# Attention loop of a decoder step: the output projection enters one loop step earlier, mixed with the end of the query projections

## The chip, the cores and the metric

One NeuronCore of a Trainium2 chip runs the whole program. The metric is the device time of one launch in microseconds; several launches of a kernel are timed, and their median is what counts. The engines named below are PE (TensorE, the matmuls), DVE (VectorE), ACT (ScalarE), POOL (GpSimd) and SP (SyncE, which here mostly issues DMA transfers). Each engine works through its own instructions in a fixed order; it waits on semaphores where an instruction needs another engine's result or a transfer.

## The reference

One inference step of a two-layer trunk on 1024 new prompt tokens and 8 sample tokens, model width 1024, all in fp32. Every layer has a mixer and a squared-ReLU MLP (width 4096), each behind an RMSNorm and added to the residual stream. Layer 0 mixes with a gated linear recurrence (RG-LRU). Layer 1 mixes with sliding-window attention, 16 query heads over 4 key/value heads of width 64, and that layer is where the change lies:

```python
q, k, v = split(x @ w_qkv)
q, k = rms_norm(q) * q_g, rms_norm(k) * k_g          # per head
s = q @ k.T / 8 - slope[head] * dist                 # keys of the own and the previous block of 128
s = where((dist >= 0) & (dist < 128), s, -1e30)
m = maximum(max(s), sink[head])
p = exp(s - m) / (sum(exp(s - m)) + exp(sink[head] - m))
y = (p @ v) @ w_out                                  # the output projection; then x = x + y
```

## The kernel before, in words

Numbers. Every fp32 product is three passes of a reduced fp32 type: each operand is split into a high part `h` and a low part `l`, and hi·hi, lo·hi and hi·lo are summed. A weight of 128x1024 that comes from DRAM into a `raw` tile is therefore split once: ACT casts the high part (L183, tile `wh`), DVE subtracts it for the low part (L184, tile `wl`), in two halves of 512 columns each. `ensure(i)` runs these splits up to weight i at the place in the program where it is called, and loads the raws of later weights (L177) behind it; a weight that has not been split when a matmul needs it is split at that place.

Tokens are the columns: 1032 of them in three chunks of 344. Activations stand with 128 channels on the partitions, so there are 8 tiles of 128 channels. The query heads are kept in 8 `q` tiles of two heads each.

The attention loop. It has 32 steps g = 0 to 31, `STEPS[g]` = (t, b): a pair of query tiles t and a block b of 128 tokens, 8 blocks for each of 4 pairs. Each step does three things, and they belong to different steps' data:

- `stage_a(g+2)`, two steps ahead (`AHEAD`): the scores, 8 matmuls (L1031) into `bSS`, of which there is a single buffer. POOL computes the distance term (L1034) into a tile `se`, scaled by factors from the query norms; DVE puts masked columns into place (L1038, not in block 0), adds scores and distance term (L1039, out of `bSS` into `se`), takes the maximum (L1040), and ACT does the exponentials (L1044). The next scores can enter `bSS` once L1039 has read it.
- `stage_b(g)`: four PE transposes of the probabilities (L1058) into the single buffer `bT`, read by ACT (L1060) and by DVE (L1062); both write `pt`. At its start POOL takes the difference of two neighbouring value blocks (L1056).
- `stage_c(g-2)`, every second step: probabilities times values and value differences (L1078) into `bO`, split by ACT (L1085) and DVE (L1086). Of the first tiles the result goes to DRAM (`od`), of the last it stays in `oh`/`ol`.

Between these, PE is given other work in small pieces, called fill steps here. `filler()` projects the query tiles 1 to 7 (L938, three matmuls a fill step, 175 fill steps in all). After each projected chunk ACT squares it (L877) and splits it (L879), DVE writes the low part (L880), and SP stores the parts to their `q` tiles (L886, L887). After a tile's last chunk `q_factors` follows: matmuls that sum the squares (L893), an ACT copy (L895), two transposes (L898), and a chain of small DVE and ACT operations (L903, L310 to L313, L315, L907, L908) that ends in the factors which POOL's distance term needs. The factors of the last tile, 7, are first needed by the scores of step 24.

The second source of fill steps, `steps`, is the output projection: for chunk 0 of the tokens and output tiles m = 0 to 3, a group of 6 fill steps over the query tiles 4, 5, 0, 1, 2, 3 (three matmuls each, L244), then the same for chunk 1; tiles 6 and 7 follow after the loop. A group ends with DVE adding the residual (L408, `x`, out of the bank `bP`). The residual tile x[m] comes back from DRAM by an SP transfer (L440), which is issued, with the split of weight wo1[m] if it hasn't been done, when the group m begins (`need(m+1)`). The attention results of tiles 0 to 3 are read back from `od` into `oh`/`ol` by L1183 before that.

What sets the order. Two tables say how many fill steps shall have been taken by which point of the loop, with straight lines between: `FILL` for the query projections up to step `G0`, `EARLY` for the output projection after it. Inside the loop the order of PE's instructions is pinned to the order of the code. For the other engines a scheduler sets the order out of the program order and the dependences, so moving a piece of code can reorder DVE, ACT and SP. Set-up of the output projection, with its L1183 loads, stands behind step G0-1.

Of the kernel before, what the change touches and what calls it, by code (L numbers as in the profile page):

```python
# [13 lines left out]
ALU = mybir.AluOpType  # L14
# [12 lines left out]
NB = SEQ // P  # L27
# [38 lines left out]
def trunk(ctx: ExitStack, tc: tile.TileContext, I, O):  # L66
    nc = tc.nc
    pe, act, dve, pool, sp = nc.tensor, nc.scalar, nc.vector, nc.gpsimd, nc.sync
# [142 lines left out]
    index = {(n, j): k for k, (n, j, _, _) in enumerate(units)}  # L211
    nloaded = [0]

    def ensure(k):
        while nloaded[0] <= min(k, len(units) - 1):
            n, j, _, alloc = units[nloaded[0]]
            fetch(nloaded[0] + (NRAW[int(n[2])] if n[:2] == "dn" else 2))
            if alloc is None:
                loaded[(n, j)] = raws[nloaded[0]]
            else:  # L220
                loaded[(n, j)] = split_unit(raws[nloaded[0]], alloc, pool if nloaded[0] in (3, 13) else dve,
                                            2 if nloaded[0] < 4 or n in ("q", "k", "v", "wo1") else 1)
            nloaded[0] += 1
# [24 lines left out]
    def run(steps):  # L248
        for _ in steps:
            pass  # L250
# [578 lines left out]
    def attention(hs):  # L829
# [123 lines left out]
        def vblk(b, p):  # L953
            h = b // 4
            o = (b % 4) * 256 + p * P
            return v_tiles[h][:, o:o + P]
# [37 lines left out]
        dvs = [se2[1][:, 516 + o:516 + o + P] for o in range(0, 4 * P, P)]  # L994
# [56 lines left out]
        def stage_b(g):  # L1051
            t, b = STEPS[g]
            se, pt = ses[g % 3], B("T")
            y = live["pt", g] = W("pt")
            if b:
                pool.tensor_tensor(dvs[g % 4], vblk(b - 1, t // 4), vblk(b, t // 4), ALU.subtract)  # L1056
            for x in range(4):
                pe.transpose(pt[:, x * P:x * P + P], se[:, x, 0:P], ident)  # L1058
                yield
            act.copy(y[:, 512:1024], pt)  # L1060
            if b:
                dve.tensor_tensor(y[:, 0:512].rearrange("p (x k) -> p x k", x=4), pt.rearrange("p (x k) -> p x k", x=4),  # L1062
                                  four(newer_t), ALU.mult)
            yield
# [136 lines left out]
        fill = filler()  # L1201

        NG = 4 * NB
        AHEAD, G0 = 2, 22
        FILL = {0: 51, 6: 90, 14: 136, G0: 177}
        EARLY = {G0 + 0.3: 0, NG: 48}
        taken = [0]

        def upto(n):
            take(n - taken[0])  # L1210

        def pace(table, g):
            at = max((k for k in table if k <= g), default=min(table))
            to = min((k for k in table if k > g), default=at)
            return table[at] if to == at else table[at] + (table[to] - table[at]) * max(0, g - at) / (to - at)

        def take(n):
            for _ in range(n):
                next(fill, None)
            taken[0] += max(n, 0)  # L1220

        def ready(g):
            t, _ = STEPS[g]
# [11 lines left out]
                run(stage_a(g))  # L1235

        for g in range(NG):
            table = FILL if g < G0 else EARLY
            place = {0: 2, 1: 1}.get((g + AHEAD) % NB, 0)
            with pinned():  # L1240
                if place == 0:
                    scores(g + AHEAD)
                if g != G0:
                    upto(int(pace(table, g + 1 / 3)))
                if g and g % 2 == 0:
                    stage_c(g - 2)
                if g == G0:
                    run(fill)
                    taken[0], fill = 0, steps
                if place == 1:  # L1250
                    scores(g + AHEAD)
                upto(int(pace(table, g + 2 / 3)))
                run(stage_b(g))
                upto(int(pace(table, g + 1)))
                if place == 2:
                    scores(g + AHEAD)
            if g == 17:
                for t in (4, 5):
                    ohl[t] = (A("oh"), A("ol"))
            if 20 <= g < 24:  # L1260
                ensure(index["wo1", g - 20])
            if g == G0 - 1:
                for t in range(4):
                    load_o(t, cs(0))
                for t in (6, 7):
                    ohl[t] = (A("oh"), A("ol"))
                srcs = [ohl[t] for t in range(8)]
                r1 = A("rt")
                rs["r1"] = r1
                xs, need, steps = out_proj("wo1", srcs, spill, "g_mlp1", r1, spill1, before=between, after=ahead(1),  # L1270
                                          early=(4, 5, 0, 1, 2, 3))
                for t in range(4):
                    load_o(t, cs(1))
            if g == 26:
                for t in range(4):
                    load_o(t, slice(2 * CH, SEQ))
# [206 lines left out]
    xs, need, steps = out_proj("wo0", gl, I["xT"], "g_mlp0", r0, spill0, before=lambda m, c: need(m + 1), after=ahead(0))  # L1483
# [146 lines left out]
```

## Time and profile before

| | |
|---|---|
| median of 3 runs | 1963.46 us (1961.69 to 1965.39) |
| the profiled execution, its time and its span | 1962.05 us, 1960.3 us |
| mean granted TensorE clock | 0.996 |
| attention loop | about 1050 to 1235 us of the span |
| PE busy over the span | 1945.4 us, 99% |

The waits list names, for an engine and line, what it waited for: microseconds in total, how many times, the longest. The window view gives a row per stretch: its bounds, its length, then busy time (and instructions) of PE, PEld, DVE, ACT and POOL, then the granted TensorE clock, the share of the DMA engines' time that is busy, and GB/s. Timeline rows have the start, the duration, engine and line, the operation, written tile and read tiles, shapes, and, in brackets, how long the engine stood idle before it and what released it. Matmuls are pipelined: consecutive rows overlap, and the distance of their starts is what one costs.

### The profile page before, as it was taken

To read this page: it belongs to the slowest core of one execution; us is meant where nothing else is said; L and a number is where in the kernel's file an instruction comes from. 1 tells how busy PE (TensorE), PEld (TensorE's weight loads), DVE (VectorE), ACT (ScalarE), POOL (GpSimd) and SP (SyncE) were. 2 spreads that over 40 slices of the span, in tenths; PEclk is the share of its full clock that TensorE was granted. 3 is DMA by queue.
4 is the path that set the end of the run, shared out by engine and by line. 5 is a ranking of instruction groups with operands and counts; after the bars stand their busy time and mean duration, and the time that the engine had idled before them with its cause. 6 is when DMAs were issued, how large, how long until landed. Compare 5 with 4: busy or idle time off the path is not lost.

```text
span 1960.3 us, 34219 instructions
## 1 busy us (share of the span) xinstructions
PE 1945.4 (99%) x12844; PEld 1812.2 (92%) x12844; DVE 1481.4 (76%) x2711; ACT 1008.5 (51%) x1993; POOL 367.8 (19%) x702
## 2 busy tenths in 40 slices
PE   9999999999999999999999999999999999999999
PEld 8999999999999899999999887999999999999998
DVE  8896737987777878778743777579877779687784
ACT  6476635543434555445554676555443436455552
POOL 2330000000000232331032666000000003223321
PEclk9999999999999999999999999999999999999999
DMA  5111242244445788888452345612444447788877
GB/s 184 44 44 54 70 165 83 109 152 157 141 157 177 229 224 236 220 202 206 130 155 81 110 112 191 210 65 103 158 144 150 148 172 263 210 201 216 233 201 181
DMA packets 115909, 308.17 MB, mean 157 GB/s; under 512 B 17560, under 2 KB 46240, under 8 KB 115744
## 3 DMA queue, kind: packets, MB, share of 16 engines
q0 software_dynamic: 30720, 104.18, 22.1%
q1 hardware_dynamic: 54496, 129.36, 20.1%
q10 hardware_dynamic: 30528, 72.45, 10.3%
q8 instruction: 101, 1.65, 0.3%
q14 instruction: 64, 0.52, 0.1%
HBM read 178.08 MB, written 115.16 MB: 150 GB/s over the span
## 4 chain that ended last, share of the span: by engine, by line
PE 92%; DVE 3%; ACT 2%; DMA 1%; issue 1%; POOL 1%; SPq 0%; DVEq 0%; ACTq 0%
PE bD L609 36%; PE bZ L609 26%; PE bP L244 11%; PE bS L244 7%; PE bT L244 3%; PE bP L938 3%; PE bSS L1031 1%; PE bO L1078 1%; PE bS L968 1%; PE bT L1058 1%; DMA x<-xT 1%; ACT se L1044 0%; DVE wl L184 0%; DMA raw<-w_out 0%; DVE sq L295 0%
## 5 line engine op out<-in xcount | busy, mean ns | idle before, releaser
L609 PEld LDWEIGHTS bD<-op,op 128*128 128x128 f32 x3072 | 380.5, 188 | 7.9
L609 PE MATMUL bD<-op,op 128*128 128x260 f32 x3072 | 383.0, 282 | 0.0
L609 PEld LDWEIGHTS bD<-tl,op 128*128 128x128 f32 x2880 | 362.4, 188 | 11.6 <-DVE ho L757 0.3
L609 PE MATMUL bD<-tl,op 128*128 128x260 f32 x2880 | 366.4, 282 | 0.1
L622 POOL DMA_DIRECT2D tl<-hsum x210 | 125.4, 682 | 886.9 <-PE bD L609 785.4
L456 ACT CAST op<-ws 128x512 fp32r<-128x512 f32 (+2 forms) x288 | 158.7, 561 | 246.9 <-DVE ws L577 114.8
L609 PE MATMUL bZ<-op,op 128*128 128x512 f32 x1152 | 282.2, 394 | 0.0
L609 PE MATMUL bZ<-tl,op 128*128 128x512 f32 x1080 | 271.8, 394 | 0.2 <-DVE tl L464 0.2
L609 PEld LDWEIGHTS bZ<-op,op 128*128 128x128 f32 x1152 | 210.4, 188 | 43.6 <-ACT he L743 0.2
L609 PEld LDWEIGHTS bZ<-tl,op 128*128 128x128 f32 x1080 | 194.4, 188 | 37.7 <-DVE tl L464 0.7
L464 DVE TENSOR_TENSOR tl<-tl 128x520 fp32r<-128x520 f32 (+1 forms) x210 | 136.4, 692 | 77.1 <-ACT tl L463 76.9
L456 ACT CAST op<-raw 128x512 fp32r<-128x512 f32 (+2 forms) x216 | 120.9, 562 | 133.9 <-PE bD L609 73.0
L457 DVE TENSOR_TENSOR op<-ws,op 128x512 fp32r<-128x512 f32 (+2 forms) x288 | 171.5, 610 | 7.3 <-ACT op L456 7.1
L457 DVE TENSOR_TENSOR op<-raw,op 128x512 fp32r<-128x512 f32 (+2 forms) x216 | 131.7, 611 | 9.3 <-ACT op L456 8.5
L757 DVE TENSOR_TENSOR ho<-bD,ho 128x520 f32<-128x520 f32 x140 | 97.5, 697 | 37.1 <-PE bD L609 36.2
L463 ACT CAST tl<-tl 128x520 fp32r<-128x520 f32 (+1 forms) x210 | 117.5, 626 | 2.1 <-DVE ho L674 0.7
L184 DVE TENSOR_TENSOR wl<-raw,wh 128x512 fp32r<-128x512 f32 (+1 forms) x73 | 63.6, 890 | 34.7 <-ACT wh L183 18.1
L747 DVE TENSOR_TENSOR ho<-bZ,ho 128x512 f32<-128x512 f32 x72 | 49.6, 689 | 44.2 <-PE bZ L609 44.0
L731 ACT COPY he<-bZ 128x512 f32<-128x512 f32 x72 | 42.0, 583 | 75.3 <-PE bZ L609 69.8
L757 DVE TENSOR_TENSOR he<-bD,he 128x520 f32<-128x520 f32 x71 | 49.4, 696 | 40.6 <-PE bD L609 40.3
L749 ACT COPY he<-bZ 128x512 f32<-128x512 f32 x68 | 39.9, 587 | 77.0 <-PE bZ L609 64.9
L183 ACT CAST wh<-raw 128x512 fp32r<-128x512 f32 (+1 forms) x76 | 57.2, 775 | 36.2 <-PE bT L244 11.3
(371 smaller groups left out, 3839.4 us busy)
## 6 DMA issues: line engine op xcount, KB each, us to landing
raw<-w_up SPq DMA_DIRECT2D x64, 512.0 KB, 3.8
tl<-hsum POOLq DMA_DIRECT2D x120, 260.0 KB, 6.7
raw<-w_dn SPq DMA_DIRECT2D x64, 384.0 KB, 6.2
tl<-hsum POOLq DMA_DIRECT2D x90, 256.0 KB, 6.3
spill<-ho POOLq DMA_DIRECT2D x32, 516.0 KB, 6.9
spill<-he POOLq DMA_DIRECT2D x32, 516.0 KB, 6.3
hsum<-ts ACTq DMA_DIRECT2D x30, 520.0 KB, 4.0
hsum<-ho ACTq DMA_DIRECT2D x30, 516.0 KB, 3.5
```

The lines of the kernel that those rows point to most:

```text
L183: act.copy(r_(hi[:, sl]), raw[:, sl])
L184: eng.tensor_tensor(r_(lo[:, sl]), raw[:, sl], hi[:, sl], ALU.subtract)
L244: pe.matmul(o, lhsT=r_(wt[:, col(k):col(k) + P]), rhs=r_(xt[:, cs(c)]), start=(k == first and a == 0), stop=(k == final and a == 2))
L456: act.copy(r_(hi), x)
L457: dve.tensor_tensor(r_(lo), x, hi, ALU.subtract)
L463: act.copy(r_(hi), lo)
L464: eng.tensor_tensor(r_(lo), lo, hi, ALU.subtract)
L609: pe.matmul(d[:, 512 * b:512 * b + c], lhsT=r_(wt[:, j * P:j * P + P]), rhs=r_(xt[:, c * b:c * b + c]), start=first and j == 0 and a == 0, ...
L622: pool.dma_start(t[:, n:2 * n], src)
L747: dve.tensor_tensor(o0, d, o[:, HP], ALU.add)
L757: last["sum"] = dve.tensor_tensor(t, inner(d), t, ALU.add).ins
L938: pe.matmul(o, lhsT=r_(wt[:, k * P:k * P + P]), rhs=r_(xt[:, cs(c)]), start=(k == 0 and a == 0), stop=(k == M8 - 1 and a == 2))
```

## The change

- `G0` goes from 22 to 21, so the output projection is set up, with its loads L1183, behind step 20 and enters the loop in step 21.
- In step G0 the kernel before ran all that was left of the query projections at once (`run(fill)`) and then went over to `steps`. Now both are merged: `mixed` takes one fill step of the one, then one of the other, until the query projections are through, and `steps` alone after that. The table for that step's end is `EARLY`.
- The numbers of `FILL` and `EARLY` are others: 92 instead of 90 fill steps at step 6, 139 instead of 136 at step 14, 176 at step 21.3; six steps of the merged source by step 22, 48 at the end of the loop.
- The splits of wo1[0] to wo1[3] are asked for behind the steps 20, 22, 24 and 26, not 20, 21, 22 and 23.
- POOL's difference of two value blocks is taken for the next step, behind the transposes, not for the own step ahead of them. Its line is L1059 now; the transposes' line is L1056.

```diff
@@ stage_b
-            if b:
-                pool.tensor_tensor(dvs[g % 4], vblk(b - 1, t // 4), vblk(b, t // 4), ALU.subtract)
             for x in range(4):
                 pe.transpose(pt[:, x * P:x * P + P], se[:, x, 0:P], ident)
                 yield
+            if (g + 1) % NB:
+                pool.tensor_tensor(dvs[(g + 1) % 4], vblk(b, t // 4), vblk(b + 1, t // 4), ALU.subtract)
             act.copy(y[:, 512:1024], pt)
@@ the loop
-        AHEAD, G0 = 2, 22
-        FILL = {0: 51, 6: 90, 14: 136, G0: 177}
-        EARLY = {G0 + 0.3: 0, NG: 48}
+        AHEAD, G0 = 2, 21
+        FILL = {0: 51, 6: 92, 14: 139, G0 + 0.3: 176}
+        EARLY = {G0 + 0.4: 0, G0 + 0.7: 3, G0 + 1: 6, NG: 48}
...
+        def mixed(a, b):
+            for _ in a:
+                yield
+                next(b)
+            yield from b
...
-            table = FILL if g < G0 else EARLY
+            table = FILL if g <= G0 else EARLY
...
-                if g != G0:
-                    upto(int(pace(table, g + 1 / 3)))
+                upto(int(pace(table, g + 1 / 3)))
                 if g and g % 2 == 0:
                     stage_c(g - 2)
                 if g == G0:
-                    run(fill)
-                    taken[0], fill = 0, steps
+                    taken[0], fill, table = 0, mixed(fill, steps), EARLY
...
-            if 20 <= g < 24:
-                ensure(index["wo1", g - 20])
+            if g in (20, 22, 24, 26):
+                ensure(index["wo1", (g - 20) // 2])
```

What that does to the order of instructions, at three places. In these rows a tile's name carries a buffer number; `x2` says that a row stands for two such instructions.

DVE where the output projection begins. Before, with wl_13129 the low part of wo1[1], wl_13240 that of wo1[2], and x_13190 the residual tile x[0]:

```order
L1062 TENSOR_TENSOR pt_13111<-bT_13110,side_10405 128x512
L184 TENSOR_TENSOR wl_13129<-raw_13055,wh_13128 128x512 x2
L903 TENSOR_TENSOR qs_13179<-bN_13119,st 128x16
L1046 RECIPROCAL den_10401<-den_10401 128x4
L1086 TENSOR_TENSOR ol_12838<-bO_13163,oh_12837 128x256
L1062 TENSOR_TENSOR pt_13197<-bT_13196,side_10405 128x512
...
L908 RECIPROCAL st<-st 128x16
L1039 TENSOR_TENSOR se_10407<-bSS_13211,se_10407 128x4x128
...
L408 TENSOR_TENSOR x_13190<-bP_13192,x_13190 128x344
```

The same place with the change; wl_13195, wl_13300 and wl_13413 are the low parts of wo1[1], wo1[2] and wo1[3], x_13147 is x[0]:

```order
L1062 TENSOR_TENSOR pt_13154<-bT_13153,side_10405 128x512
L903 TENSOR_TENSOR qs_13174<-bN_13140,st 128x16
L408 TENSOR_TENSOR x_13147<-bP_13149,x_13147 128x344
L184 TENSOR_TENSOR wl_13195<-raw_13065,wh_13194 128x512 x2
L1046 RECIPROCAL den_10401<-den_10401 128x4
...
L908 RECIPROCAL st<-st 128x16
L184 TENSOR_TENSOR wl_13300<-raw_13192,wh_13299 128x512 x2
L1086 TENSOR_TENSOR ol_12875<-bO_13206,oh_12874 128x256
L1062 TENSOR_TENSOR pt_13223<-bT_13222,side_10405 128x512
L1086 TENSOR_TENSOR ol_12877<-bO_13206,oh_12876 128x256
L184 TENSOR_TENSOR wl_13413<-raw_13297,wh_13412 128x512 x2
L1039 TENSOR_TENSOR se_10407<-bSS_13237,se_10407 128x4x128
```

The split of wo1[1] moved from ahead of the first group's residual add L408 to behind it, and three weights' splits now stand within eleven instructions, the last of them directly ahead of the add L1039 that frees `bSS`.

PE there, with the change (bP_13149 is the bank of group m = 0, bP_13202 that of m = 1). Before, the 4 matmuls L893 were followed by stage_c (L1078), L898 and then group 0, and scores stood between the groups:

```order
L1031 MATMUL bSS_13102<-kl_10745,q_12192 128x256
L893 MATMUL bN_13140<-sq_12860,con 32x256 x4
L244 MATMUL bP_13149<-oh_12874,wh_13067 128x344
...
L1056 MATMUL bT_13153<-con,se_10407 128x128 x4
...
L898 MATMUL bN_13140<-con,qc_13141 128x128 x2
...
L244 MATMUL bP_13149<-oh_13085,wl_13068 128x344
L244 MATMUL bP_13202<-oh_12874,wh_13194 128x344
L244 MATMUL bP_13202<-ol_12875,wh_13194 128x344
L244 MATMUL bP_13202<-oh_12874,wl_13195 128x344
L1078 MATMUL bO_13206<-pt_13051,vt_10403 64x256 x2
```

Group 0, the transposes of step 21 and the end of the query factors are woven into one another, all 18 matmuls of group 0 and three of group 1 stand ahead of stage_c of step 20, and the third of group 1 reads wl_13195.

DVE at a block 0 in the middle of the loop, and near its end. Before, the L184 pair of that query weight stood 15 instructions later, and the mask copy of the late scores was followed by L1062:

```order
L1062 TENSOR_TENSOR pt_11982<-bT_11981,side_10405 128x512
L1039 TENSOR_TENSOR se_10408<-bSS_11996,se_10408 128x4x128
...
L1038 COPY_PREDICATED bSS_13499<-side_10405,bSS_13499 128x4x128
L1062 TENSOR_TENSOR pt_13477<-bT_13476,side_10405 128x512
L1039 TENSOR_TENSOR se_10408<-bSS_13499,se_10408 128x4x128
```

With the change:

```order
L1062 TENSOR_TENSOR pt_11989<-bT_11988,side_10405 128x512
L184 TENSOR_TENSOR wl_12076<-raw_11752,wh_12075 128x512 x2
L1039 TENSOR_TENSOR se_10408<-bSS_12003,se_10408 128x4x128
...
L1038 COPY_PREDICATED bSS_13514<-side_10405,bSS_13514 128x4x128
L1046 RECIPROCAL den_10400<-den_10400 128x4
L1039 TENSOR_TENSOR se_10408<-bSS_13514,se_10408 128x4x128
L1062 TENSOR_TENSOR pt_13492<-bT_13491,side_10405 128x512
```

A split of a query weight stands ahead of the add that frees `bSS`, and late in the loop the read of `bT` stands behind that add instead of ahead of it.

## The prediction

> **What bounds the kernel now.** I read the busy times first, then PE's waits, then windows and timelines around the two waits that lie in the attention loop.
>
> ```profile
> PE 1945.4 (99%) x12844; PEld 1812.2 (92%) x12844; DVE 1481.4 (76%) x2711; ACT 1008.5 (51%) x1993; POOL 367.8 (19%) x702
> PE bSS L1031 <- DVE se L1039: 4.3, 2, 3.5
> PE bO L1078 <- DVE pt L1062: 1.3, 1, 1.3
> ```
>
> PE is the bound. The change removes no matmul and adds none, so only PE's waits and its clock can move. Inside the loop PE waits 5.6 us on DVE. Most of that is in one place, where the output projection begins:
>
> ```profile
> 1186.97 0.65 PE L1078 MATMUL bO<-pt,se 128*64 128x256 f32 x4 [1.30 <-DVE pt L1062]
> 1191.22 0.32 PE L244 MATMUL bP<-ol,wh 128*128 128x344 f32 x1
> 1191.38 0.32 PE L244 MATMUL bP<-oh,wl 128*128 128x344 f32 x1
> 1195.16 0.58 PE L1031 MATMUL bSS<-kh,q 128*128 128x256 f32 x1 [3.47 <-DVE se L1039]
> ...
> 1193.21 0.25 DVE L908 RECIPROCAL st<-st 128x16 f32<-128x16 f32 x1
> 1194.42 0.69 DVE L1039 TENSOR_TENSOR se<-bSS,se 128x512 f32<-128x512 f32 x1 [0.95 <-POOL se L1034]
> ```
>
> The 3.47 us are the chain of tile 7's factors: L908 ends at 1193.46, POOL's distance term follows, DVE's add then frees the scores' only buffer. What comes behind the wait is in the windows:
>
> ```profile
> 1187.50:1191.70 4.20, 4.20 (x31) 3.84 (x29) 2.66 (x8) 2.95 (x12) 2.87 (x7) 1.00 0.97 277
> 1191.70:1194.30 2.60, 0.00 (x0) 0.00 (x0) 1.72 (x5) 0.50 (x1) 0.67 (x2) 1.00 1.01 404
> 1194.30:1201.10 6.80, 5.94 (x24) 5.88 (x25) 5.21 (x12) 3.65 (x11) 3.75 (x13) 0.50 1.02 383
> ```
>
> After 2.60 us without a matmul the granted clock falls to 0.50 and stays there for 6.80 us. PE is busy for 5.94 of them at half speed, so 2.97 us are lost. The DMA engines are full here (0.97 to 1.02), which will matter.
>
> **What the change takes away.** With the query projections' end mixed into step 21, tile 7's factors start about one step earlier against the scores that need them, and stage_c of step 20 stands behind group 0 rather than directly behind the transposes. Both waits lose their cause: 1.30 + 3.47 = 4.77. With the 3.47 goes its half-clock stretch, 2.97. **Gain: 7.74 us**, if nothing takes their place.
>
> **C1, the wait of group m = 1 for wo1[1]'s low part.** This is the largest cost. The order rows show that DVE makes wl_13195 behind the residual add L408 of group 0. That add needs x[0], whose SP transfer is issued only when group 0 begins; before the change the low part was made ahead of all that. When does PE reach the third matmul of group 1? Take PE's old track and correct it by what now stands elsewhere:
>
> ```profile
> 1184.16 0.65 PE L1078 MATMUL bO<-pt,vt 128*64 128x256 f32 x4
> 1187.56 0.44 PE L898 MATMUL bN<-con,qc 128*128 128x128 f32 x2
> 1188.31 0.60 PE L1058 MATMUL bT<-con,se 128*128 128x128 f32 x4
> 1188.66 0.41 PE L244 MATMUL bP<-oh,wh 128*128 128x344 f32 x1
> 1189.70 0.22 PE L1031 MATMUL bSS<-kh,q 128*128 128x128 f32 x1
> 1190.54 0.37 PE L244 MATMUL bP<-oh,wh 128*128 128x344 f32 x1
> ```
>
> The 15th projection matmul of the old track ends its slot at 1191.38 + 0.16 = 1191.54. Away go the wait (1.30), stage_c (1187.56 - 1184.16 - 1.30 = 2.10), one set of transposes (0.35) and the scores (0.84); five more projection matmuls come in (20 stand before the waiting one), 5 x 0.16 = 0.80. PE arrives at 1187.75.
>
> And the low part?
>
> ```profile
> 1178.24 0.53 SPq L1183 DMA_DIRECT2D ol<-od0l  x1
> 1183.08 0.43 SPq L1183 DMA_DIRECT2D oh<-od2h  x1
> L440 SPq DMA_DIRECT2D x<-spill x8: 319/376/384, 1188.7 to 1227.0; - x8
> DMA to landing us min/median/max: 3.9/5.5/7.5
> 1198.13 0.52 DVE L408 TENSOR_TENSOR x<-bP,x 128x344 f32<-128x344 f32 x1 [0.16 <-PE bP L244]
> 1182.80 1.31 DVE L184 TENSOR_TENSOR wl<-raw,wh 128x512 fp32r<-128x512 f32 x2
> ```
>
> SP's queue is in order, and in the changed program a row of 13 of the loads L1183 stands directly ahead of x[0]. Ten steps from 1178.24 to 1183.08 take 4.84, 0.48 each; 13 of them bring x[0]'s issue to 1184.5. These transfers land 3.9 to 7.5 us after issue, median 5.5; with the DMA engines full I take 6.0, so x[0] is there at 1190.5. The add (0.52 here) and two halves of the split (1.31) follow: 1192.3. C1 is therefore 4.55 less whatever has delayed PE before (C2): with the bounds of the landing 2.45 to 6.05 for both together.
>
> **C2, the last squares.** L893 reads the squares of tile 7's last chunk. On ACT these stand behind a copy out of `bT`, a cast of stage_c and both halves of wo1[0]'s cast:
>
> ```profile
> 1183.75 0.59 ACT L1060 COPY pt<-bT 128x512 f32<-128x512 f32 x1
> 1188.01 0.35 ACT L1085 CAST oh<-bO 128x256 fp32r<-128x256 f32 x1
> 1181.54 1.15 ACT L183 CAST wh<-raw 128x512 fp32r<-128x512 f32 x2
> 1183.02 0.46 ACT L877 ACTIVATE sq<-bP 128x344 f32<-128x344 f32 x1 [0.33 <-PE bP L938]
> ```
>
> That is 0.59 + 0.35 + 1.15 + 0.46 = 2.55 from the transposes on, while PE has six projection matmuls (0.96) and eight scores to do (0.12 apart at full width, 0.96), 1.92. The difference and some 0.3 until a copy starts give 0.9, bounds 0 and 1.6. It is no cost on top: C1 shrinks by it, to 3.65. **C1 + C2 = 4.55.**
>
> **C3, scores of step 25.** From the transposes of step 22 on, DVE waits about 1.0 for ACT's copy, as the 0.59 of the copy and its start make it, and then has L1062, L1086, two halves of a split and the scores' add: 0.7 + 0.4 + 1.3 + 0.7, together 4.1 us. PE has nine projection matmuls (1.44), the narrow scores of step 24 (0.84) and three more (0.48), 2.76 us, before the next scores: a wait of 1.4. If the clock is halved there, PE takes 5.5 and the wait is nil. I take 0, bound 1.4.
>
> **C4, late transposes.** In one late step DVE now does L1039 before it reads `bT`:
>
> ```profile
> 1216.94 0.67 DVE L1038 COPY_PREDICATED bSS<-side,bSS 128x512 f32<-128x512 int32 x1
> 1217.52 0.68 DVE L1062 TENSOR_TENSOR pt<-bT,side 128x512 f32<-128x512 f32 x1
> 1218.12 0.68 DVE L1039 TENSOR_TENSOR se<-bSS,se 128x512 f32<-128x512 f32 x1
> 1218.35 0.63 PE L1058 MATMUL bT<-con,se 128*128 128x128 f32 x4
> ```
>
> Already now the transposes start 0.15 after L1062's end (1218.20). With L1039 and a reciprocal between, that end moves 0.7 later, and PE, with three projection matmuls fewer in between, comes 0.48 sooner: 1.2 to 1.4. I take 1.3, bounds 0 and 1.4.
>
> **C5, splits of query weights.** At scores 8 PE has no slack at all:
>
> ```profile
> 1108.74 0.68 DVE L1039 TENSOR_TENSOR se<-bSS,se 128x512 f32<-128x512 f32 x1
> 1109.47 0.39 PE L1031 MATMUL bSS<-kh,q 128*128 128x256 f32 x1
> 1137.62 1.40 DVE L184 TENSOR_TENSOR wl<-raw,wh 128x512 fp32r<-128x512 f32 x2
> ```
>
> The next scores start 0.05 after the add's end. The new order puts a pair of halves ahead of such an add (1.3), and another pair ahead of a mask copy further on, where more PE work lies between (0.8, half of it covered). Together 2.1, bounds 0 and 2.8.
>
> **C6, the clock again.** A wait of 3.65 is longer than the 2.60 of empty PE behind which the clock fell. 1.05 us of a halved stretch of 6.80 would then pass in the wait, 5.75 in work: 2.9 lost, bounds 0 and 3.4. The Trainium skill ("TensorE: Matmul & The Clock Gate", section "HAM oscillation — how this bites in real kernels") puts the limit at idle gaps of more than about 3.4 us; the gap of this trace, 3.47, is just above it. By that figure C6 would be paid as well, but only just.
>
> POOL's value difference costs nothing: POOL is busy 19%, and the product that reads it comes at least a step later. If that cover were gone, it would be one such instruction per step ahead of the distance term.
>
> **Sum.** -7.74 + 4.55 + 0 + 1.3 + 2.1 + 2.9 = +3.1. Against the profiled execution's own 1962.05 us that is 1965.2; this execution lies 1.4 below the median of the runs, so **I forecast 1966.6 us**.
>
> **Rivals.** *The clock holds.* If x[0] lands in the median 5.5, C1 is 3.15, and if the clock then isn't lowered, C6 is nil and C3 is paid: -7.74 + 4.05 + 1.4 + 1.3 + 2.1 = +1.1, 1964.6. Against it speaks the fall after 2.60 us of no work, and another one that needed no empty PE at all:
>
> ```profile
> 1275.79 2.40 PE L1152 MATMUL bN<-ssb,vc 128*128 128x8 f32 x20
> 1279.60:1286.50 6.90, 6.90 (x28) 6.90 (x27) 2.48 (x12) 1.75 (x6) 0.00 (x0) 0.51 0.07 27
> ```
>
> Twenty tiny matmuls preceded it. The page's limit would separate 3.15 from 3.65, so by it this case is a matter of half a microsecond in the landing of one transfer.
>
> *DVE is early (faster).* If x[0] lands after 3.9, as the fastest did, the low part is ready at 1190.2, C1 + C2 is 2.45 and the clock holds; if the pairs of halves then also meet an idle DVE (busy 76%), C4 and C5 vanish: -7.74 + 2.45 + 1.4 = -3.9, 1959.6. It decides at a wait of less than 2.6 in group 1. The missing slack at scores 8 speaks against it.
>
> *The loads come late (slower by more).* Three raws of w_out and the x tiles are now wanted within one step, on DMA engines that are full. If x[0] needs 7.5, C1 + C2 is 6.05; and if wo1[2]'s raw takes the longest time that this kind took, the splits ahead of L1086, L1062 and L1039 stand about 2 us longer and all of DVE's queue with them:
>
> ```profile
> DMA to landing us min/median/max: 3.1/4.5/8.5
> ```
>
> That row is of the raws, L177: 8.5 against 4.5. +3.1 + 1.5 + 2.0 = +6.6, 1970.1. For it speak the 404 GB/s of the empty stretch; against it, that the loads of `oh`/`ol` start a step earlier and so free the queue earlier.
>
> That the change doesn't do what it says is excluded for the mixing (the order shows it), but not for the splits: called two steps apart, they still stand within eleven DVE instructions.
>
> **How the numbers follow.** Forecast 0.46, the clock holds 0.17, DVE early 0.22, loads late 0.15. A measurement here can't tell less than about 0.2%, 3.9 us, from no change: faster is below 1959.5, slower above 1967.4. The forecast's own range, 1964 to 1969, lies 0.28 within and 0.18 above; the clock's case is within (0.17); DVE early sits on the lower bound (0.13 faster, 0.09 within); late loads are above (0.14, 0.01 within). Faster 0.13, the same 0.55, slower 0.32. The range runs from 1959.5 to 1970, which leaves out about half of either outer case, 0.2 in all.
>
> **What would show it.** Right: no wait of L1031 on L1039 in step 22 above 1 us and none of L1078; a wait of 3 to 4 us of PE at L244 in group 1, released by DVE's L184; x[0]'s L440 issued near 1184.5 less the earlier gains, landing after the group's last matmul; a clock of about 0.5 behind it; waits of L1031 near scores 8, of the transposes late. Wrong: group 1 without a wait (x[0] early, or the low part ahead of L408 after all), or a granted clock of 1.00 through the whole loop.

## The result

The changed kernel takes 1970.01 us (median of 7 runs, 1966.91 to 1972.92); the kernel before, timed on the same chip in the same rounds, 1963.12 us (7 runs, 1960.59 to 1965.39). The ratio is 1.0035, 95% interval 1.0023 to 1.0047: slower by 6.9 us, 0.35%, clear of no change. The forecast was 1966.6 us, 3.1 more than the kernel before, and the range ran from 1959.5 to 1970: the measured time lies on its upper end. The direction was right, the rise more than twice the forecast one, and of the prediction's own chances a loss that can be seen had 0.32, none that can be seen 0.55.

The profiled execution of the changed kernel took 1968.33 us, its span is 1966.5 us, 6.2 more than the span before. PE's busy time is the same to 0.4 us, and its waits are others. First the busy times and the list of PE's waits with the change:

```profile
PE 1945.8 (99%) x12844; PEld 1808.4 (92%) x12844; DVE 1481.2 (75%) x2711; ACT 1007.4 (51%) x1993; POOL 364.2 (19%) x702
...
PE bP L244 <- DVE wl L184: 5.0, 1, 5.0
PE bSS L1031 <- DVE se L1039: 2.9, 3, 1.2
PE bT L1056 <- DVE pt L1062: 1.9, 2, 1.3
...
PE bN L893 <- ACT sq L877: 0.7, 1, 0.7
...
PE bT L1056 <- DVE q L313: 0.4, 1, 0.4
```

The two waits that the kernel before had at the output projection's beginning, 1.30 and 3.47 us, are gone. In their place stands one of 5.0 us, on the instruction that the prediction named: the third matmul of group 1, for wo1[1]'s low part. In the timelines of PE, DVE and SP:

```profile
1191.51 0.31 PE L244 MATMUL bP<-ol,wh 128*128 128x344 f32 x1
1196.81 0.66 PE L244 MATMUL bP<-oh,wl 128*128 128x344 f32 x1 [4.98 <-DVE wl L184]
1205.62 0.38 PE L1031 MATMUL bSS<-kh,q 128*128 128x256 f32 x1 [1.23 <-DVE se L1039]
...
1195.04 0.52 DVE L408 TENSOR_TENSOR x<-bP,x 128x344 f32<-128x344 f32 x1 [3.72 <-DMA x<-spill]
1195.47 1.28 DVE L184 TENSOR_TENSOR wl<-raw,wh 128x512 fp32r<-128x512 f32 x2
...
1187.51 0.38 SPq L440 DMA_DIRECT2D x<-spill  x1
```

It is read from the bottom up: x[0] is asked for at 1187.51 and lands 7.4 us later; DVE stands at L408 for 3.72 us and starts it at 1195.04, 7.5 us after the issue; then come the add and the two halves of the split, and PE goes on at 1196.81. The windows show the clock behind it (length, then busy PE, PEld, DVE, ACT, POOL; granted clock; DMA share; GB/s):

```profile
1187.80:1191.80 4.00, 4.00 (x28) 3.71 (x26) 3.42 (x9) 3.13 (x9) 1.57 (x5) 1.00 0.97 327
1191.80:1193.90 2.10, 0.03 (x1) 0.00 (x0) 0.00 (x0) 1.46 (x7) 0.00 (x0) 1.00 1.09 244
1193.90:1200.70 6.80, 3.89 (x17) 2.01 (x17) 3.89 (x10) 1.14 (x2) 3.58 (x10) 0.50 0.84 269
```

The clock fell 2.1 us into the wait and was half for 6.8 us again, but 2.9 of these passed in the wait itself.

The waits ahead of step 20 and late in the loop, in PE's timeline, with the two rows of DVE that make the first of them wait, a split ahead of the add that frees `bSS`:

```profile
1111.69 0.39 PE L1031 MATMUL bSS<-kh,q 128*128 128x256 f32 x1 [0.98 <-DVE se L1039]
1129.38 0.65 PE L1078 MATMUL bO<-pt,se 128*64 128x256 f32 x4 [0.24 <-DVE pt L1062]
1147.06 0.63 PE L1056 MATMUL bT<-con,se 128*128 128x128 f32 x4 [0.37 <-DVE q L313]
1155.60 0.39 PE L1031 MATMUL bSS<-kh,q 128*128 128x256 f32 x1 [0.73 <-DVE se L1039]
1177.60 0.63 PE L1056 MATMUL bT<-con,se 128*128 128x128 f32 x4 [0.59 <-DVE pt L1062]
...
1226.22 0.63 PE L1056 MATMUL bT<-con,se 128*128 128x128 f32 x4 [1.32 <-DVE pt L1062]
1294.42 0.43 PE L244 MATMUL bP<-ol,wh 128*128 128x344 f32 x1 [0.44 <-DVE ol L272]
...
1109.75 1.28 DVE L184 TENSOR_TENSOR wl<-raw,wh 128x512 fp32r<-128x512 f32 x2
1110.95 0.68 DVE L1039 TENSOR_TENSOR se<-bSS,se 128x512 f32<-128x512 f32 x1
```

### The profile page after: what moved, and what is told of

Read it like the earlier page. It is cut to its first block, busy times and chain, and to the rows that moved or that the text cites. A ratio compares the mean times of both kernels' runs of the same rounds, so it can differ in the third digit from the quotient of the medians.

```text
span 1966.5 us, 34229 instructions
## 1 busy us (share of the span) xinstructions
PE 1945.8 (99%) x12844; PEld 1808.4 (92%) x12844; DVE 1481.2 (75%) x2711; ACT 1007.4 (51%) x1993; POOL 364.2 (19%) x702
## 4 chain that ended last, share of the span: by engine, by line
PE 91%; DVE 4%; ACT 2%; DMA 1%; issue 1%; SPq 0%; POOL 0%; ACTq 0%; DVEq 0%
PE bD L609 36%; PE bZ L609 26%; PE bP L244 11%; PE bS L244 7%; PE bT L244 3%; PE bP L938 3%; PE bO L1078 1%; PE bSS L1031 1%; PE bS L968 1%; ACT se L1044 1%; PE bT L1056 1%; DVE wl L184 1%; DMA raw<-w_in 1%; DVE sq L295 0%; DMA tl<-hsum 0%
## 5 line engine op out<-in xcount | busy, mean ns | idle before, releaser
L184 DVE TENSOR_TENSOR wl<-raw,wh 128x512 fp32r<-128x512 f32 (+1 forms) x73 | 63.6, 888 | 36.6 <-ACT wh L183 19.9
```

The lines of the kernel that those rows point to most:

```text
L184: eng.tensor_tensor(r_(lo[:, sl]), raw[:, sl], hi[:, sl], ALU.subtract)
```

## The experiments

Eleven kernels were run. They were timed in three groups, each with the kernel before beside them on the same chip; its medians there were 1963.23, 1963.60 and 1963.37 us, and a ratio is to the kernel before of the same group. Single runs of one kernel scatter by 4 to 10 us, so that a difference of less than about 2 us between two kernels can't be told. The question was which part of the change costs what, and whether it is an order on DVE (theory A) or full DMA engines that make something late anyway (theory B).

### The split of wo1[1] asked for earlier

```diff
             if g in (20, 22, 24, 26):
-                ensure(index["wo1", (g - 20) // 2])
+                ensure(index["wo1", max(1, (g - 20) // 2)])
```

> The changed kernel with the split of wo1[1] asked for behind step 20, together with wo1[0]'s, so that DVE makes its low part ahead of the residual add L408. Theory A (order: the low part of wo1[1] stands behind L408, which waits for x[0]): the 5.0 us wait of L244 on L184 goes, with it the half clock behind it (about 2.0 us), and, since DVE's order there changes too, the 1.2 us of L1031 in the next step and the 1.3 us of the late transposes: about 9.5 us less, 1960.5 us. Theory B (transfers: the DMA engines are full there, so PE will wait for the next thing that comes late, wo1[2]'s raw or the attention results): the wait moves to group 2 or to the oh/ol tiles and keeps 3 us or more, with the half clock; less than 4 us gained, 1966 us or more.

Measured: 1968.05 us, 1.0022 of the kernel before (1.0013 to 1.0031). The 5.0 us wait is gone, as both theories of its cause had it, but only about 2 us of time with it, hardly more than can be told. PE waits at other places: 1.76 us for the last squares (L893), which now stand behind two more halves of a cast on ACT, 1.61 us at the scores of step 25, 1.15 at late transposes. The profiled execution is the slowest of the eleven (1971.57 us); in it the scores of step 9 wait 2.71 us, a part of it for a transfer issue on ACT (below, under hardware), and a half clock of 3.4 us follows that wait and another the 1.76 us. Theory A was right on the wait, wrong on the time. The time is theory B's, but not in its way: no wait of 3 us or more stands at group 2 or at the `oh`/`ol` tiles.

### x[0] asked for earlier

```diff
+                need(1)
                 for t in range(4):
                     load_o(t, cs(1))
```

> The changed kernel with x[0]'s load issued ahead of the second row of eight loads L1183, so some 3.8 us earlier; DVE's order is as in the changed kernel. Theory A: x[0] lands 3.8 us earlier, the wait of L244 on L184 shrinks from 5.0 to about 1.2 us, no half clock behind it: 5.8 us less, 1964.2 us. Theory B: on full DMA engines an earlier issue lands hardly earlier; the wait stays above 3.5 us and the time within 2 us of the changed kernel's 1970.

Measured: 1966.15 us, 1.0016 (1.0006 to 1.0025). In this kernel's profile:

```profile
1184.15 0.38 SPq L440 DMA_DIRECT2D x<-spill  x1
...
1191.38 0.52 DVE L408 TENSOR_TENSOR x<-bP,x 128x344 f32<-128x344 f32 x1
...
1193.15 0.42 PE L244 MATMUL bP<-oh,wl 128*128 128x344 f32 x1 [1.50 <-DVE wl L184]
1201.41 0.39 PE L1031 MATMUL bSS<-kh,q 128*128 128x256 f32 x1 [2.54 <-DVE se L1039]
...
1196.03 1.14 ACT L183 CAST wh<-raw 128x512 fp32r<-128x512 f32 x2 [2.72 <-DMA raw<-w_out]
```

Only the issue was moved, by 3.4 us, and the wait fell from 4.98 to 1.50 with no half clock behind it: x[0]'s place in SP's queue is what made group 1 wait. So far theory A; what theory B expected, an early issue that lands hardly earlier, did not come, since x[0] took 5.1 us to land here and 7.4 in the changed kernel. But the scores of step 25 now wait 2.54 us instead of 1.23, and a half clock of 3.4 us follows: ACT stands 2.72 us for the raw of wo1[2], DVE's split of it follows, and behind that split stands the add for the scores. ACT's wait for that raw is not new, it is 4.18 us in the changed kernel; there PE itself came to these scores 5.5 us later (1204.39 instead of 1198.87). By the medians some 3.9 us of the expected 5.8 came; the rest was given back to the transfer that is late next.

### The old pace of the query projections

```diff
-        FILL = {0: 51, 6: 92, 14: 139, G0 + 0.3: 176}
+        FILL = {0: 51, 6: 90, 14: 136, G0 + 0.3: 176}
```

> The changed kernel with the pace of the query projections as before: 90 fill steps at step 6 and 136 at step 14, where the change has 92 and 139. All else as changed. The splits of the query weights are again where they were, behind the scores' add; and in the order that the scheduler then makes, wo1[1]'s low part stands ahead of L408, and the read of bT late in the loop ahead of L1039. Theory A: the waits of 0.98, 0.24, 0.37 and 0.59 us in the steps before 20 go (2.1 us), the 5.0 with its half clock (2.0), the 1.2 and the 1.3 too: about 11.5 us less, 1958.5 us, faster than the kernel before. Theory B: only the 2.1 us in the early steps go, the transfers keep PE waiting in groups 1 and 2: 1967 us.

Measured: 1961.09 us, 0.9993 (0.9984 to 1.0002), no difference from the kernel before that can be told; against the changed kernel's 1.0035 that is some 8 us less. Two numbers of the pace undo the whole loss, with the mixing, the later splits and the moved value difference all left in. The 5.0 us are 0.73 us here, since the low part stands ahead of L408 in DVE's order. Three larger waits are left: 2.00 us at the scores of step 9 behind a slow issue on ACT (below, under hardware), 1.16 at the late transposes, for POOL (L1048) now instead of L1062, and 2.57 at the scores of step 25 again. The rows of the order and of the last of these:

```profile
1188.93 1.28 DVE L184 TENSOR_TENSOR wl<-raw,wh 128x512 fp32r<-128x512 f32 x2
1193.25 0.52 DVE L408 TENSOR_TENSOR x<-bP,x 128x344 f32<-128x344 f32 x1 [3.04 <-PE bP L244]
...
1195.04 1.14 ACT L183 CAST wh<-raw 128x512 fp32r<-128x512 f32 x2 [2.05 <-DMA raw<-w_out]
1195.69 1.29 DVE L184 TENSOR_TENSOR wl<-raw,wh 128x512 fp32r<-128x512 f32 x2 [0.74 <-ACT wh L183]
1197.84 0.68 DVE L1039 TENSOR_TENSOR se<-bSS,se 128x512 f32<-128x512 f32 x1
1198.58 0.38 PE L1031 MATMUL bSS<-kh,q 128*128 128x256 f32 x1 [2.57 <-DVE se L1039]
```

The expected 1958.5 is missed by 2.6 us; theory A had none of these three waits.

### The value difference back at its old place

```diff
+            if b:
+                pool.tensor_tensor(dvs[g % 4], vblk(b - 1, t // 4), vblk(b, t // 4), ALU.subtract)
             for x in range(4):
...
-            if (g + 1) % NB:
-                pool.tensor_tensor(dvs[(g + 1) % 4], vblk(b, t // 4), vblk(b + 1, t // 4), ALU.subtract)
```

> The changed kernel with POOL's value difference at its old place, at the start of the step that uses it. Theory: POOL is busy 19% and nothing of the product waits for this difference; DVE's order stays as changed, so 1970 us, within 1 us. Rival: the difference ahead of the transposes delays POOL's distance term and so the scores' add, or its move was what freed it: 2 us or more either way.

Measured: 1971.24 us, 1.0032 (1.0022 to 1.0041), the same as the changed kernel, with the same waits (4.42, 1.22, 1.32 us). In the changed kernel this part costs and brings nothing that can be measured.

### The new pace alone, on the kernel before

```diff
-        FILL = {0: 51, 6: 90, 14: 136, G0: 177}
+        FILL = {0: 51, 6: 92, 14: 139, G0: 177}
```

> The kernel before with nothing but the changed pace of the query projections: 92 fill steps at step 6 and 139 at step 14 instead of 90 and 136. DVE's order in the early steps is then that of the changed kernel, a pair of L184 halves ahead of the scores' add. Theory A: PE waits of about 1.0, 0.2, 0.4 and 0.6 us appear in the steps before 20, and the two old waits at the start of the output projection stay: 2.1 us more than before, 1965.3 us. Rival: the early waits only take PE time that the later 1.3 and 3.5 us waits would take anyway (the chain of tile 7's factors then has more room): no difference, 1963 us.

Measured: 1968.01 us, 1.0026 (1.0015 to 1.0038): 4 to 5 us slower, most of the change's loss by itself and more than either theory had. The early waits are there (1.08, 0.23, 0.37 us, then 0.51 and 0.54 at two transposes). They are 2.7 us together by the list; by PE's progress they cost more, since the first matmul of group 0, with the same work done before it in both kernels, starts at 1191.72 instead of 1187.75, 4.0 us later. And the old wait of 3.47 us grew by 1.4:

```profile
1195.33 0.62 ACT L183 CAST wh<-raw 128x512 fp32r<-128x512 f32 x1 [2.74 <-DMA raw<-w_out]
...
1195.98 0.69 DVE L184 TENSOR_TENSOR wl<-raw,wh 128x512 fp32r<-128x512 f32 x1 [3.19 <-ACT wh L183]
1196.96 0.23 DVE L313 SCALAR_TENSOR_TENSOR q<-qs,st,q 128x16 f32<-128x16 f32 x1
1198.60 0.25 DVE L908 RECIPROCAL st<-st 128x16 f32<-128x16 f32 x1
1200.54 0.58 PE L1031 MATMUL bSS<-kh,q 128*128 128x256 f32 x1 [4.88 <-DVE se L1039]
...
1189.70 0.53 SPq L177 DMA_DIRECT2D raw<-w_out  x1
```

Here the chain of tile 7's factors (L313 to L908) stands behind a half of wo1[2]'s split, which waits for that weight's raw. In the kernel before, its first operation stood ahead of that half:

```profile
1190.50 0.43 DVE L313 SCALAR_TENSOR_TENSOR q<-qs,st,q 128x16 f32<-128x16 f32 x1
1191.71 0.69 DVE L184 TENSOR_TENSOR wl<-raw,wh 128x512 fp32r<-128x512 f32 x1 [0.77 <-ACT wh L183]
```

The raw was issued at 1189.70; before it was at 1185.12. There are two raw buffers, so wo1[2]'s raw can be asked for only when wo1[0]'s split is through, and with the new pace that split ends at 1188.1 instead of 1184.1. But PE is 4.0 us later there as well: against PE the half of the split starts only 0.3 us later. The other 1.1 us are order: from the start of that half to the end of L908 DVE takes 2.87 us instead of 1.75, with L1086, L313 and the read of `bT` (L1062) between them now. So it is again the order on DVE, more than the transfer, that links the pace of the earlier steps with a wait in step 22.

### The splits again one step apart, with the old pace

```diff
-            if g in (20, 22, 24, 26):
-                ensure(index["wo1", (g - 20) // 2])
+            if 20 <= g < 24:
+                ensure(index["wo1", g - 20])
```

> As the changed kernel with the old pace, and also with the splits of wo1[0] to wo1[3] asked for behind the steps 20, 21, 22 and 23 as before. What is left of the change is the mixing in step 21 with its earlier set-up, and POOL's value difference. Theory A: the first two splits stand where they stood with the old pace alone, so the same waits at group 1 (0.7 us) and at the scores of step 25 (2.6 us with a half clock of 3.4 us behind it): the same time, 1961 us. Rival: the splits two steps apart are what leaves the scores of step 25 waiting; then 2 to 4 us less, 1957 to 1959 us.

Measured: 1961.94 us, 0.9995 (0.9987 to 1.0004); waits of 0.70 us in group 1 and 2.54 at the scores of step 25. As theory A has it, the distance of the splits does nothing here.

### The splits a step earlier, with the old pace

```diff
-            if g in (20, 22, 24, 26):
-                ensure(index["wo1", (g - 20) // 2])
+            if 19 <= g < 23:
+                ensure(index["wo1", g - 19])
```

> As the changed kernel with the old pace, and the splits of wo1[0] to wo1[3] asked for behind the steps 19, 20, 21 and 22. The two raw buffers come free a step earlier, so that the raws of wo1[1] and wo1[2] are loaded ahead of the rows of loads L1183 and behind x[0]. Theory A (the wait of 2.6 us of step 25's scores is DVE held up by the split of wo1[2], whose raw lands late): that wait falls below 1 us and its half clock goes, about 3.5 us less than with the old pace alone: 1957.5 us. Theory B (the DMA engines are full, so a load moved ahead makes another late): a wait of 2 us or more elsewhere in steps 21 to 25, 1961 us.

Measured: 1960.59 us, 0.9988 (0.9980 to 0.9997): by its interval just faster than the kernel before. In its profile, in step 21 and after:

```profile
1179.64 0.38 SPq L177 DMA_DIRECT2D raw<-w_out  x1
...
1190.41 1.42 DVE L184 TENSOR_TENSOR wl<-raw,wh 128x512 fp32r<-128x512 f32 x2 [0.53 <-ACT wh L183]
1194.80 1.31 DVE L184 TENSOR_TENSOR wl<-raw,wh 128x512 fp32r<-128x512 f32 x2 [0.47 <-ACT wh L183]
...
1184.94 0.63 PE L893 MATMUL bN<-sq,con 128*32 128x256 f32 x4 [1.38 <-ACT sq L877]
1196.77 0.39 PE L1031 MATMUL bSS<-kh,q 128*128 128x256 f32 x1 [1.51 <-DVE se L1039]
```

With wo1[0] split earlier its buffer is free earlier, wo1[2]'s raw is issued at 1179.64, and its split (1190.41) no longer holds up the scores' add; the one that stands ahead of that add now is wo1[3]'s (1194.80). The wait fell from 2.57 to 1.51 and no half clock follows. The last squares wait more for it (1.38 instead of 0.43). Between the two theories: the named wait shrank by the named cause, yet not below 1 us, and against the old pace alone the gain, 0.5 us by the medians, can't be told from none.

### wo1[0] split two steps earlier, with the old pace

```diff
-            if g in (20, 22, 24, 26):
-                ensure(index["wo1", (g - 20) // 2])
+            if g in (18, 20, 21, 22):
+                ensure(index["wo1", {18: 0, 20: 1, 21: 2, 22: 3}[g]])
```

> As the changed kernel with the old pace, and the splits of wo1[0] to wo1[3] asked for behind the steps 18, 20, 21 and 22. Same question as in the run with 19, 20, 21 and 22, with wo1[0]'s raw buffer free another step earlier; in DVE's order a half of wo1[3]'s split stands ahead of the add that the scores of step 25 wait for. Theory A: 1 us for that half, else as there: 1958.5 us. Theory B: 1961 us.

Measured: 1961.36 us, 0.9987 (0.9979 to 0.9996), the same as the run before it and theory B's number, with 1.61 us at the scores of step 25. These two are the only kernels of the study whose interval lies below the kernel before: by 0.12 and 0.13%, some 2.5 us, with upper ends of 0.9997 and 0.9996.

### One number of the pace at a time

```diff
-        FILL = {0: 51, 6: 92, 14: 139, G0 + 0.3: 176}
+        FILL = {0: 51, 6: 90, 14: 139, G0 + 0.3: 176}
```

> The changed kernel with 90 fill steps at step 6 as before, but still 139 at step 14. In DVE's order the early pairs of L184 stand behind the scores' add again, except one half ahead of a mask copy, while the low part of wo1[1] still stands behind L408, wo1[3]'s still ahead of the add of step 24, and the late read of bT still behind L1039. Theory A: the early waits (0.98, 0.24, 0.37, 0.59 us) go, the 5.0 with its half clock, the 1.2 and the 1.3 stay: 2 us less than the changed kernel, 1968 us. Rival (the early waits are what makes the later ones, by bringing PE and the loads out of step): 1963 us or less.

```diff
-        FILL = {0: 51, 6: 92, 14: 139, G0 + 0.3: 176}
+        FILL = {0: 51, 6: 92, 14: 136, G0 + 0.3: 176}
```

> The changed kernel with 136 fill steps at step 14 as before, but 92 at step 6. Here DVE's order keeps the pair of L184 ahead of the add of scores 8, while wo1[1]'s low part stands ahead of L408 and the late read of bT ahead of L1039, as with the old pace. Theory A: the wait of about 1.0 us at scores 9 stays, the 5.0 us go and the others are as with the old pace: 1 us above that one's 1961, 1962.3 us. Rival: 1967 us or more.

Measured: 1967.19 us, 1.0022 (1.0013 to 1.0031), with only step 6 back; 1965.39 us, 1.0010 (1.0001 to 1.0020), with only step 14 back. The first is theory A's number, the second lies between its theory and its rival. The order on DVE separates as expected: in the first the wait of L244 for L184 stays (4.66 us), in the second it is 0.72 us. So it is the number at step 14 that puts wo1[1]'s low part behind L408, with no edit near that place. The early waits don't separate so cleanly. In the first kernel they were expected to go and stayed in other places (0.81 and 0.60 us at transposes, 0.90 at scores); in the second there are more of them than expected (0.59, 0.80, 0.34). In both profiles a slow issue on ACT adds to the wait at the scores of step 9 (1.31 and 2.31 us). What the pace costs early in the loop, and at which scores, is left open in detail.

### The new pace with the splits a step earlier

```diff
-            if g in (20, 22, 24, 26):
-                ensure(index["wo1", (g - 20) // 2])
+            if 19 <= g < 23:
+                ensure(index["wo1", g - 19])
```

> The changed kernel with its new pace, and the splits of wo1[0] to wo1[3] asked for behind the steps 19, 20, 21 and 22. DVE makes the low part of wo1[1] well ahead of L408 then; one half of wo1[2]'s stands behind it. Theory A: the early waits stay (2.1 us), the 5.0 us with its half clock go, the scores of step 25 wait about 1.5 us: what the same splits gave with the old pace (1960.6) and 2.1 on top, 1962.7 us. Rival (the pace itself costs more than its early waits): 1966 us or more.

Measured: 1966.70 us, 1.0022 (1.0012 to 1.0031), the rival's number. Group 1 no longer waits. The transfer of x[0] holds DVE all the same, and the wait has moved to the scores of step 25:

```profile
1190.23 0.53 SPq L440 DMA_DIRECT2D x<-spill  x1
...
1196.21 0.52 DVE L408 TENSOR_TENSOR x<-bP,x 128x344 f32<-128x344 f32 x1 [3.14 <-DMA x<-spill]
1199.42 1.28 DVE L184 TENSOR_TENSOR wl<-raw,wh 128x512 fp32r<-128x512 f32 x2
1200.62 0.68 DVE L1039 TENSOR_TENSOR se<-bSS,se 128x512 f32<-128x512 f32 x1
1201.36 0.58 PE L1031 MATMUL bSS<-kh,q 128*128 128x256 f32 x1 [3.24 <-DVE se L1039]
```

The instruction that stands in DVE's queue and waits for x[0] is the same L408; only what queues behind it is other. Removing the 5.0 us at group 1 in this way left 3.24 us there and the half clock of 6.8 us.

## Why the prediction was right or wrong

**The gain.** Both old waits went and their half clock with them, 7.74 us as forecast. All of it, and 6 us more, came back. With the old pace both are gone too, and there mainly 2.57 + 2.00 + 1.16 + 0.73 us of other waits and 1.7 us of a half clock took their place: the gain came and was spent again, all of it or nearly.

**C1 and C2, 4.55 forecast, 5.70 measured** (4.98 + 0.72). The mechanism is the one named, instruction by instruction: the 13 loads ahead of x[0], the add L408, the split, the third matmul of group 1. The run with x[0] earlier shows that the queue is the cause. The prediction had x[0] issued at 1184.5 and PE at the third matmul 4.15 us later; it was 1187.51 and 4.32 us later, both some 3 us behind the old track. What was mis-sized is the landing: 7.5 us until the add could start, the top of the bounds, where the prediction chose 6.0. That the DMA engines were full was seen in the windows (0.97 to 1.02); the choice should have leaned to the slow end.

**C3, 0 forecast, 1.23 measured.** The wait itself had been worked out as 1.4, by the chain that came, and was then struck out because the clock would be half there. That step failed: the clock was back at full at 1200.7, before these scores (1205.62). The half stretch was 6.8 us long as before and began in the wait, and the longer wait used up more of it.

**C4, 1.3 forecast, 1.32 measured.** DVE's L1039 ahead of the read of `bT`, in the step named.

**C5, 2.1 forecast, 2.07 measured** (0.98 + 0.24 + 0.37 + 0.59, less 0.11 that the wait of 0.84 lost), but only the 0.98 is at a place that the prediction gave. Right in sum, partly by luck, and by the listed figures only: in the run with the pace alone the early waits of 2.7 us by the list made PE 4.0 us late.

**C6, 2.9 forecast, about 2.0 measured**: half of the 3.9 us of work that the half clock covered.

**Not in the sum**: 0.44 us at L244 after the loop, for a low part that DVE makes at L272 (it is in six of the eleven experiments too); a gain of 1.7 us where the half clock behind the tiny matmuls lasted 3.4 instead of 6.8 us, which hangs on where they lie in the clock's grid (last section) and not on the change. By these figures the span should have grown by -7.74 + 5.70 + 1.23 + 1.32 + 2.07 + 2.0 + 0.44 - 1.7 = 3.3; it grew by 6.2. The remaining 2.9 us are not in a wait that the profile lists. Two thirds of them lie inside the attention loop, where PE stops in six places more than before, and a stop costs more than its listed wait. The wait is counted from the end of the row before it: that row at 1191.51 is 0.31 us long, where the next start follows after 0.16 otherwise; and behind the wait at 1205.62 the next start follows after 0.22 us, where 0.12 is usual. By such starts each of the stops in the loop cost 0.2 to 0.6 us on top, for the six more some 1.5 us, an estimate. Where the other 1.4 us went was not found.

**The larger mistake** is not a term but what the terms were read from. The prediction took the 4.55 and the 2.9 from the order rows of the finished change, and did not ask which of the edits made that order; its text speaks of the mixing and the set-up a step earlier, and of the pace not at all. The runs show: mixing, earlier set-up, later splits and value difference together, with the old pace, are within the noise of the kernel before (0.9993, and 0.9995 with the splits one step apart as well), and the pace alone costs 0.26% on the kernel before.

**The rivals.** The clock did not hold. DVE was not early. Late loads were the rival that came nearest: 1970.1 forecast for it, and x[0] did need 7.5 us. That its number is the measured one is partly luck: its second half, 2.0 us for a late raw of wo1[2], did not come as a wait of PE. The raw was late (it landed 6.7 us after its issue, and ACT waited 4.18 us), but PE was late by then itself; in the experiments that raw holds up the scores of step 25 once x[0] is out of the way.

**The rule on the clock.** The Trainium skill ("TensorE: Matmul & The Clock Gate", section "HAM oscillation — how this bites in real kernels") has the clock fall at idle gaps of more than about 3.4 us. The runs here don't agree: it fell behind waits of 1.75 us and of 2.3 to 2.7 us too. The prediction took the trace's 2.60 over the page's figure, which was the right choice.

## What to carry to other kernels

A pace table changed by two or three fill steps of half a microsecond can reorder other engines many steps later, where a scheduler fills in their order; so of a change with several numbers the order should be built for each number alone, and the one that moves a split behind an instruction that waits for a transfer is the one to pay attention to. Where a kernel's engine waits for a transfer in the middle of its queue, taking the waiting consumer away does not take the wait away: with the new pace, three runs removed the 5.0 us wait or cut it to 1.5 and found 1.6 to 3.2 us at the scores of step 25 instead. What shortened that wait, with the old pace, was to free the buffer earlier, so that the transfer itself could start (2.57 us fell to 1.51 and 1.61); the gain in time over the old pace alone can't be told from none.

## What the hardware showed that was not expected

**The clock is decided on a grid.** In every profile of the study all edges of the half-clock stretches between 1040 and 1340 us lie whole multiples of 3.413 us apart: in the changed kernel the falls and rises are at 1193.92, 1200.74, 1286.08 and 1289.49, the last three 2.00, 27.00 and 28.00 units (of 3.413 us) from the first, in the run with the split of wo1[1] earlier they are up to 53.00 units apart. The stretches are 3.41, 6.83 or, once, 10.24 us long. Over all profiles:

| PE's wait, us | half clock behind it |
|---|---|
| 1.50, 1.51, 1.57, 1.61, 1.61 | none |
| 1.75, 1.76 | 3.41 us |
| 1.79, 2.00 | none |
| 2.31, 2.54, 2.54, 2.57, 2.71 | 3.41 us |
| 3.24, 3.47, 4.42, 4.66, 4.88, 4.98 | 6.83 us |

What separates 1.75 from 2.00 is how the wait lies in the grid. Adding up PE's idle time grid unit by grid unit, in all thirteen profiles from 50 to 1950 us, the clock fell behind 13 units in which PE had waited, and PE was idle for 1.75 to 3.41 us in each; among the units behind which it stayed full none has more than 1.61 us. The 1.75 us of the run with the splits again one step apart lie in one unit, PE is busy for 1.67 of its 3.41 us, and the clock falls at its end. The 2.00 us of the run with the old pace are divided, 1.39 and 0.60:

```profile
1108.55:1111.96 3.41, 1.67 (x12) 1.39 (x11) 2.30 (x4) 0.93 (x2) 0.23 (x1) 1.00 0.34 95
...
1107.13:1110.54 3.41, 2.02 (x16) 1.74 (x14) 1.23 (x3) 0.93 (x2) 0.98 (x3) 1.00 0.22 69
1110.54:1113.95 3.41, 2.81 (x21) 2.77 (x21) 2.82 (x6) 1.78 (x7) 0.37 (x1) 1.00 0.41 100
```

In these runs the clock thus fell when PE was idle for about half of a unit. Once it was half, less kept it there: it stayed half behind units with 0.66 to 2.89 us of idle PE and rose behind those with none or 0.54, so the waits of 3.24 us and more cost two units here. This is read off the thirteen profiles; no run moved a wait within the grid on purpose.

**Tiny matmuls lower the clock without any wait**: behind the 128x8 matmuls of the sample part (L1152) the half clock lasted 6.83 us before, 3.41 in the changed kernel, 10.24 in one experiment and none in five others, with no edit there. That alone is up to 5 us between profiles, half of 10.24. The same grid sorts these cases: in the eight profiles with a half clock there, 18 to 22 of the 32 matmuls started in the unit ahead of the fall; in the five without, no unit holds more than 17. That these matmuls count as little work for the clock is what the numbers suggest; no run changed them.

**An issue on ACT can take 2 us.** In six of the thirteen profiles one or two of the transfers that ACT issues (L1089) took 1.1 to 2.2 us to issue instead of 0.35, and ACT's next work stood behind them. In the run with the old pace:

```profile
1106.55 2.24 ACTq L1089 DMA_DIRECT2D od1l<-o  x1
1108.83 0.45 ACT L879 CAST hi<-bP 128x344 fp32r<-128x344 f32 x1 [2.77 <-issue]
1111.14 0.39 PE L1031 MATMUL bSS<-kh,q 128*128 128x256 f32 x1 [2.00 <-DVE se L1039]
```

The kernel before has the same instruction at 0.37 us and no wait at these scores. What makes it slow was not found.
